# Two single PSUM banks for the third GEMM tile of the SSD mixer

## The chip, the cores and the metric

The kernel runs on one core of one Trainium2 chip. The metric is the device time of one execution in microseconds (us), taken as the median of several runs. The profile used here comes from one further execution of the same program, recorded by the hardware profiler. The engines are named as the profile names them: PE is TensorE (matrix products), PEld its weight loads, DVE is VectorE, ACT is ScalarE, POOL is GpSimd, and SP is SyncE, whose queue issues the DMAs.

## The reference

Two layers work on 512 latent tokens with 256 context tokens in front, at model width 1024, in fp32. Layer 0 mixes tokens by attention, layer 1 by a bidirectional Mamba-2 mixer (SSD). A gated convolutional FFN follows each. The change lies in the SSD mixer, which computes, cut to its core:

```
h_lat, h_ctx           # modulated RMS norms, 512 and 256 tokens x 1024
z, xbc, dt = split(h @ w_in, widths 2048, 4096, 64)
xbc = silu(dwconv_centred(xbc, w, b))   # 5 taps over positions, latent and context apart
x, B, C = split(xbc)                    # 32 heads of 64 in 8 groups, state of 128
dt = softplus(dt + bias);  a = -exp(a_log)
# in both directions, in chunks of 128 tokens:
h_t = exp(dt_t a) h_{t-1} + dt_t B_t x_t ;  y_t = C_t h_t
y = (y_fwd + y_bwd + D x) * silu(z)
out = rms_norm(y) @ w_out               # added through a gate to the stream
```

The context runs through the state only: it starts the recurrence of the latent tokens, and of x and B it needs all 768 positions, of C and z only the latent 512.

## The kernel before

Features lie on the 128 partitions and tokens along the free axis. An fp32 product is made of three passes (`mm3`): with input and weight each split into a high and a low part, the rows of TensorE with L105 multiply high by high, L106 the low input by the high weight, L108 the high input by the low weight. `load_w` brings one weight tile of 128x1024 from memory (`wst`, a DMA in SyncE's queue), ScalarE casts the high part (`wh`, L85), and VectorE subtracts it for the low part (`wl`, L87). All three buffers come from one rotation of ten.

A GEMM tile of the SSD input projection makes 128 output features from eight k-steps: for latent tokens 8 x 3 matmuls of 512 columns, for context 8 x 3 of 256. The result lies in PSUM. PSUM is given out by two pools: `S`, two tiles of two banks each (1024 columns), and `B`, four tiles of a single bank (512 columns), from which `Bank` takes. A tile of a pool can be taken again once what was in it has been read by its last reader.

The mixer begins with `first_tiles`, which computes two GEMM tiles while the preceding norm is still being finished: the time steps (`ps_dt`) and the first x tile (`ps_x0`). Both are `S` tiles, and the profile calls both `ps_first`. ScalarE then reads the time steps in four passes (L914 and L915, twice each, the rows `dte` and `dt`), VectorE and ScalarE make the softplus and its running sums (`acs`, L935 and L936). `inproj` runs over the 8 groups. For each group it makes the tiles x0, x1, B, C, z0 and z1, in that order; group 0 takes its x0 from `first_tiles`, so that its x1 is the third GEMM tile of the mixer. `gemm` takes an `S` tile for each, called `ps_in`, and computes the context part ahead of the latent part. With both `S` tiles taken by the time steps and x0, x1 of group 0 takes the one of the time steps.

`conv` evicts a tile: ScalarE copies the latent columns (L955) and, for x and B, the context columns (L957) into a padded buffer `raw`, of which there are two, multiplies by the middle tap (L958), VectorE adds the other four taps (L960), and ScalarE applies SiLU (L964). In group 0, after C, the sums of the time steps are transposed to tokens (`ps_dtT`, copied by VectorE at L1136 into `acsT` and `dtT`), spread by a product (`ps_end`, L1141), and turned into decays (`dec`, `dw`). `core` then works on a group: it transposes x (`ps_xt`, L1004) and B (`ps_bt`), weights x (`xw`, L1018), makes the products of C and B (`ps_cb`) and the states (`ps_st`, L1030), the decay masks `E`, and from them `ps_yo` and `ps_y`, while `inproj` already works on the next group.

Behind the groups comes the output projection: `ysplit` splits each gated tile into high and low parts (L1180 on ScalarE, L1181 on VectorE; `hhy` and `hly` for the first eight tiles, `yh` and `yl` for the rest), and `ps_wo` are its products. The FFN follows.

Outside attention the order on each engine isn't written out by hand. A list scheduler sets it from the dependencies and its estimates of durations, when the program is built; pools then assign the buffers, and each engine executes its instructions in the order given.

Of the kernel before, what the change touches and what calls it, by code (L numbers as in the profile page):

```python
# [17 lines left out]
L = 512  # L18
C = 256
T = L + C  # L20
# [47 lines left out]
def t3(g, name, dt=F32, n=T):  # L68
    return g.t3p.tile([P, n], dt, tag="t3", bufs=g.n3, name=name)
# [20 lines left out]
def load_w(g, dram, lo_engine="dve", pin=False):  # L90

    st = t4(g, "wst")
    wh = t4(g, "wh", F32R)
    wl = t4(g, "wl", F32R)
    g.nc.sync.dma_start(st, dram)
    split(g, st, wh, wl, lo_engine=lo_engine, pin=pin)
    return wh, wl


def mm3(g, w, outs, first, last):  # L100

    wh, wl = w
    mm = g.nc.tensor.matmul
    for out, (ah, al) in outs:
        mm(out, wh, ah, start=first, stop=False)  # L105
        mm(out, wh, al, start=False, stop=False)  # L106
    for out, (ah, al) in outs:
        mm(out, wl, ah, start=False, stop=last)  # L108
# [106 lines left out]
def follow(g, bi):  # L215

    if g.last_act is not None:
        g.tc.add_manual_dep(bi.ins, g.last_act.ins.name, mybir.DependencyInfo(
            mybir.DependencyClass.NoSync, mybir.DependencyReason.DATA), reason="order of tables")
    g.last_act = bi  # L220
# [81 lines left out]
def S(g, name):  # L302
    return g.ps.tile([P, 1024], F32, tag="S", bufs=2, name=name)


def Bank(g, name):
    return g.ps.tile([P, 512], F32, tag="B", bufs=4, name=name)
# [44 lines left out]
def gemm_in(g, tiles, h, off, segs):  # L352


    for run in segs:
        for ps, w in tiles:
            for k in range(KT):
                ks = slice(k * P, (k + 1) * P)
                mm3(g, (w[0][:, ks], w[1][:, ks]),
                    [(ps[:, off[i] + a : off[i] + b], tuple(t[:, a:b] for t in h[i][k])) for i, a, b in run],  # L360
                    k == 0, k == KT - 1)
                yield
# [6 lines left out]
def first_tiles(g, ws, norm, bg):  # L369

    ends = ending(norm.streams)
    tiles = [(S(g, "ps_first"), w) for w in ws]
    for _ in gemm_in(g, tiles, norm.h, (0, L), [[s] for s in ends]):
        next(bg, None)
    for _ in bg:
        pass
    return [ps for ps, _ in tiles]
# [498 lines left out]
def ssd(g, x, norm, wf, bg, close):  # L876


    nc, I, tc = g.nc, g.I, g.tc
    par = lambda name, j, rows=P: g.par[:rows, PC[name] + j : PC[name] + j + 1]  # L880
    h = norm.h
    ps_dt, ps_x0 = first_tiles(g, wf, norm, bg)
# [14 lines left out]
    def gemm(w, streams):  # L897
        ps = S(g, "ps_in")
        for _ in gemm_in(g, [(ps, w)], h, (0, L), [[(i, 0, (L, C)[i])] for i in streams]):
            pass  # L900
        return ps
# [3 lines left out]
    ps = ps_dt  # L905
# [45 lines left out]
    def conv(ps, j, both, cv):  # L951
        raw = raws[raw_n[0] % 2]
        raw_n[0] += 1
        n = TW if both else L
        nc.scalar.copy(raw[:, 2 : 2 + L], ps[:, :L])  # L955
        if both:
            nc.scalar.copy(raw[:, L + 4 : L + 4 + C], ps[:, L:T])  # L957
        nc.scalar.activation(cv, raw[:, 2 : 2 + n], AF.Identity, scale=par("sw2", j), bias=par("sb", j))  # L958
        for tap in (0, 1, 3, 4):
            i = nc.vector.scalar_tensor_tensor(cv, raw[:, tap : tap + n], par(f"sw{tap}", j), cv, ALU.mult, ALU.add)  # L960
            while late:
                g.tc.add_manual_dep(i.ins, late.pop().ins.name, mybir.DependencyInfo(
                    mybir.DependencyClass.NoSync, mybir.DependencyReason.DATA), reason="PSUM first")
        follow(g, nc.scalar.activation(cv, cv, AF.Silu))  # L964
        return cv
# [4 lines left out]
    def inproj(gi):  # L970

        G = Group()
        ld = lambda i: load_w(g, I["win"][6 * gi + i])
        G.x = []
        for j in range(2):
            ps = ps_x0 if gi == j == 0 else gemm(ld(j), (1, 0))
            G.x.append(conv(ps, 2 * gi + j, True, t3(g, "xf")))
            yield G
        for name, i, st in (("B", 2, (1, 0)), ("C", 3, (0,))):
            ps = gemm(ld(i), st)  # L980
            yield None
            setattr(G, name, conv(ps, 8 * i + gi, i == 2, t3(g, "Bf") if i == 2 else t2("Cf")))
            yield G
        G.z = []
        for j in range(2):
            ps = gemm(ld(4 + j), (0,))
            z = t2("z")
            follow(g, nc.scalar.activation(z, ps[:, :L], AF.Silu))
            G.z.append(z)
            yield G  # L990
# [129 lines left out]
    for gi in range(8):  # L1120
        i = -1
        for G in inproj(gi):
            if G is None:
                next(prev, None)
# [79 lines left out]
    for kp in range(8):  # L1204
        w = load_w(g, I["wout0"][kp])
        if kp == 4:
            ws, ps = wm(4), Bank(g, "ps_wo")
# [19 lines left out]
    for m in range(4, KT):  # L1227
# [5 lines left out]
        for seg in SEGS[0] if m == KT - 1 else [(0, 0, L)]:  # L1233
            _, a, b = seg
            if m > 4:
                ps = Bank(g, "ps_wo")[:, : b - a]
# [203 lines left out]
```

## Time and profile before

| | us |
|---|---|
| runs | 1898.59, 1896.82, 1892.41 |
| median | 1896.82 |
| profiled execution | 1896.57 |
| its span, first to last instruction | 1894.8 |
| PE busy | 1864.3 |
| DVE busy | 1315.9 |
| ACT busy | 811.8 |
| POOL busy | 302.6 |
| mean granted TensorE clock | 0.994 of full speed |

In a row of the timeline stand the start, the length, the engine, the line in the kernel, the operation, output and inputs by the names of the program, and a count if several like it follow; in brackets the idle time just ahead of it and the instruction that ended this. Several matmuls overlap in TensorE's pipeline, so the distance of their starts, not the length of a row, is what one of them takes. Lines of helpers (L85 to L108) stand for all their callers; the tile names tell these apart.

### The profile page before, as it was taken

How to read it: one execution, taken by the hardware profiler on the slowest of the kernel's cores; microseconds unless marked ns; L12 is line 12 of the kernel's file. 1: busy time of each engine (PE TensorE's matmuls, PEld its weight loads, DVE VectorE, ACT ScalarE, POOL GpSimd, SP SyncE). 2: the span in 40 equal slices, each digit the busy share in tenths (PEclk: the TensorE clock that was granted, in tenths of full speed). 3: DMA queues.
4: the chain of work that ended last, by engine and by line, in shares of the span. 5: the costliest groups of instructions: out<-in, count | busy, mean ns of one | idle time of the engine just before them, and what ended most of it. 6: DMA issues, size and time to landing. Idle time of an engine off the chain costs nothing.

```text
span 1894.8 us, 28684 instructions
## 1 busy us (share of the span) xinstructions
PE 1864.3 (98%) x11426; PEld 1549.6 (82%) x11426; DVE 1315.9 (69%) x1949; ACT 811.8 (43%) x1410; POOL 302.6 (16%) x266
## 2 busy tenths in 40 slices
PE   9999999999999999999999999999999999999999
PEld 7876565688888888888888888888888878888887
DVE  6587778688877776444477877777787466565655
ACT  4544443364221222222366676776666352323331
POOL 2241120040000000000041334444333210000000
PEclk9999999999999999999999999999999999999999
DMA  9232441115443553222224323334353223223232
GB/s 341 81 105 62 134 153 37 34 57 189 145 133 124 183 183 123 67 67 67 67 90 122 120 83 120 118 121 125 122 161 107 79 78 100 98 81 110 89 101 89
DMA packets 74070, 211.67 MB, mean 112 GB/s; under 512 B 9040, under 2 KB 14544, under 8 KB 73808
## 3 DMA queue, kind: packets, MB, share of 16 engines
q1 hardware_dynamic: 73936, 209.84, 33.7%
q8 instruction: 90, 1.47, 0.3%
q14 instruction: 44, 0.36, 0.1%
HBM read 198.79 MB, written 6.82 MB: 109 GB/s over the span
## 4 chain that ended last, share of the span: by engine, by line
PE 82%; DVE 10%; issue 4%; ACT 2%; POOL 1%; DMA 1%; POOLq 0%; SPq 0%; DVEq 0%; ACTq 0%
PE ps_up L106 10%; PE ps_up L108 10%; PE ps_up L105 10%; PE ps_d L105 6%; PE ps_d L106 6%; PE ps_d L108 6%; PE ps_in L108 4%; PE ps_in L106 4%; PE ps_in L105 4%; PE ps_s L672 2%; PE ps_o L636 2%; PE ps_st L1030 2%; DVE ht L281 1%; PE ps_wo L108 1%; PE ps_wo L105 1%
## 5 line engine op out<-in xcount | busy, mean ns | idle before, releaser
L87 DVE TENSOR_TENSOR wl<-wst,wh 128x1024 fp32r<-128x1024 f32 x207 | 259.8, 1255 | 235.9 <-PE ps_up L106 137.3
L85 ACT CAST wh<-wst 128x1024 fp32r<-128x1024 f32 x211 | 221.2, 1049 | 400.9 <-DMA wst<-in_wup 328.9
L106 PE MATMUL ps_up<-hlf,wh 128*128 128x512 f32 (+1 forms) x1008 | 357.0, 354 | 0.0
L108 PE MATMUL ps_up<-hhf,wl 128*128 128x512 f32 (+1 forms) x1008 | 356.8, 354 | 0.0
L105 PE MATMUL ps_up<-hhf,wh 128*128 128x512 f32 x1008 | 356.8, 354 | 0.0
L106 PEld LDWEIGHTS ps_up<-hlf,wh 128*128 128x128 f32 x1008 | 190.6, 189 | 26.3
L105 PEld LDWEIGHTS ps_up<-hhf,wh 128*128 128x128 f32 x1008 | 190.5, 189 | 26.5
L108 PEld LDWEIGHTS ps_up<-hhf,wl 128*128 128x128 f32 x1008 | 190.5, 189 | 26.4
L105 PE MATMUL ps_in<-hhs,wh 128*128 128x512 f32 (+1 forms) x560 | 204.4, 365 | 1.2 <-ACT dt L915 1.2
L106 PE MATMUL ps_in<-hls,wh 128*128 128x512 f32 (+1 forms) x560 | 199.4, 356 | 0.0
L108 PE MATMUL ps_in<-hhs,wl 128*128 128x512 f32 (+1 forms) x560 | 198.7, 355 | 0.0
L105 PE MATMUL ps_d<-hdh,wh 128*128 128x512 f32 (+1 forms) x568 | 193.5, 342 | 0.2 <-ACT hdh L85 0.2
L108 PE MATMUL ps_d<-hdh,wl 128*128 128x512 f32 (+1 forms) x568 | 193.4, 341 | 0.0
L106 PE MATMUL ps_d<-hdl,wh 128*128 128x512 f32 (+1 forms) x568 | 192.9, 340 | 0.3 <-DVE hdl L87 0.3
L781 DVE SCALAR_TENSOR_TENSOR X<-ps_d,mod,X 128x512 f32<-128x512 f32 (+1 forms) x224 | 124.5, 585 | 35.2 <-PE ps_d L108 35.0
L105 PEld LDWEIGHTS ps_in<-hhs,wh 128*128 128x128 f32 x560 | 105.9, 189 | 16.3 <-ACT dt L915 1.4
L106 PEld LDWEIGHTS ps_d<-hdl,wh 128*128 128x128 f32 x568 | 106.7, 188 | 14.8 <-DVE hdl L87 0.7
L108 PEld LDWEIGHTS ps_in<-hhs,wl 128*128 128x128 f32 x560 | 105.8, 189 | 14.8
L108 PEld LDWEIGHTS ps_d<-hdh,wl 128*128 128x128 f32 x568 | 106.7, 188 | 13.1
L105 PEld LDWEIGHTS ps_d<-hdh,wh 128*128 128x128 f32 x568 | 106.3, 188 | 13.6 <-ACT hdh L85 0.7
L106 PEld LDWEIGHTS ps_in<-hls,wh 128*128 128x128 f32 x560 | 106.0, 189 | 13.2
L675 ACT ACTIVATE pr<-ps_s 128x1024 f32<-128x1024 f32 x56 | 57.2, 1021 | 109.8 <-PE ps_s L674 104.6
(344 smaller groups left out, 3675.2 us busy)
## 6 DMA issues: line engine op xcount, KB each, us to landing
wst<-in_wup SPq DMA_DIRECT2D x88, 512.0 KB, 3.3
wada<-in_adaT SPq DMA_DIRECT2D x56, 512.0 KB, 3.3
wst<-in_win SPq DMA_DIRECT2D x48, 512.0 KB, 3.4
wst<-in_wdown SPq DMA_DIRECT2D x44, 512.0 KB, 3.9
E<-ad SPq DMA_DIRECT2D x64, 256.0 KB, 6.0
wada<-in_adaB SPq DMA_DIRECT2D x24, 512.0 KB, 4.2
ec<-ead SPq DMA_DIRECT2D x64, 128.0 KB, 5.0
wst<-in_wout SPq DMA_DIRECT2D x16, 512.0 KB, 3.4
```

The lines of the kernel that those rows point to most:

```text
L85: keep(nc.scalar.copy(hi, src))
L87: keep(eng.tensor_tensor(lo, src, _r(hi), ALU.subtract))
L105: mm(out, wh, ah, start=first, stop=False)
L106: mm(out, wh, al, start=False, stop=False)
L108: mm(out, wl, ah, start=False, stop=last)
L281: nc.vector.scalar_tensor_tensor(t[:, c0:c1], ap, g.moda[layer][ca][:, m, v : v + 1], rs[:, c0:c1], ALU.mult, ALU.mult)
L636: nc.tensor.matmul(po[S64[e], :n], v, pr[:, 512 * e + off : 512 * e + off + n], start=first, stop=last)
L672: nc.tensor.matmul(outs[e], kk[e][a][S64[e], k], b[S64[e], q], start=i == 0, stop=False)
L675: nc.scalar.activation(pr, ps, AF.Exp)
L781: nc.vector.scalar_tensor_tensor(ap, o[:, c0:c1], gate[:, m, v : v + 1], ap, ALU.mult, ALU.add)
L1030: nc.tensor.matmul(ps[:, d * 256 : (d + 1) * 256], Bt[:, t * P : (t + 1) * P], xw[d][t], start=t == ts[0], stop=t == ts[-1])
```

## The change

x1 of group 0 no longer takes an `S` tile. It takes two tiles of the `B` pool, one for the latent columns and one for the context columns, and its two parts are computed one after the other, the context first. `conv` takes such a pair too, and copies each part from its own bank. Both are called `ps_in1` in the code; in the order below `ps_in_9692` is the context part and `ps_in_9691` the latent part. Lines behind the first edit move by 1, behind the second by 7.

```
-        nc.scalar.copy(raw[:, 2 : 2 + L], ps[:, :L])
+        pl, pc = (ps[0], ps[1][:, :C]) if isinstance(ps, list) else (ps[:, :L], ps[:, L:T])
+        nc.scalar.copy(raw[:, 2 : 2 + L], pl)
         if both:
-            nc.scalar.copy(raw[:, L + 4 : L + 4 + C], ps[:, L:T])
+            nc.scalar.copy(raw[:, L + 4 : L + 4 + C], pc)
...
         for j in range(2):
-            ps = ps_x0 if gi == j == 0 else gemm(ld(j), (1, 0))
+            if gi == 0 and j == 1:
+                w, ps = ld(j), [Bank(g, "ps_in1"), Bank(g, "ps_in1")]
+                for i in (1, 0):
+                    for _ in gemm_in(g, [(ps[i], w)], h, (0, 0), [[(i, 0, (L, C)[i])]]):
+                        pass
+            else:
+                ps = ps_x0 if gi == j == 0 else gemm(ld(j), (1, 0))
             G.x.append(conv(ps, 2 * gi + j, True, t3(g, "xf")))
```

The scheduler sets another order from there on. On TensorE, where the last latent k-steps of the two first tiles stand (`hhs` and `hls` are the high and low parts of the normed input), the difference reads:

```order
 L108 MATMUL ps_first<-hhs_7_4729,wl 128x256
+L105 MATMUL ps_in_9692<-hhs_0_4731,wh 128x256
+L106 MATMUL ps_in_9692<-hls_0_4732,wh 128x256
 L105 MATMUL ps_first<-hhs_0_4715,wh 128x256 x2
+L108 MATMUL ps_in_9692<-hhs_0_4731,wl 128x256
+L105 MATMUL ps_in_9692<-hhs_1_4733,wh 128x256
+L106 MATMUL ps_in_9692<-hls_1_4734,wh 128x256
+L108 MATMUL ps_in_9692<-hhs_1_4733,wl 128x256
 L106 MATMUL ps_first<-hls_0_4716,wh 128x256
 L108 MATMUL ps_first<-hhs_0_4715,wl 128x256
```

Six matmuls of the context part of x1 now stand among the products of the first tiles; the other 18, and the latent part, follow behind the last of these.

On ScalarE, where x0, x1, B and C of group 0 are evicted, the order before (`xf` with L964 are the SiLUs of x0 and x1, `raw_9668` receives B, `raw_9669` C):

```order
L964 ACT_TABLE_LOAD
L964 ACTIVATE xf<-xf 128x770
L955 COPY raw_9668<-ps_in 128x512
L957 COPY raw_9668<-ps_in 128x256
L958 ACTIVATE Bf<-raw_9668,par 128x770
L964 ACTIVATE xf<-xf 128x770
L85 CAST wh<-wst 128x1024
L955 COPY raw_9669<-ps_in 128x512
L958 ACTIVATE Cf<-raw_9669,par 128x512
```

and now:

```order
L965 ACT_TABLE_LOAD
L965 ACTIVATE xf<-xf 128x770 x2
L956 COPY raw_9668<-ps_in 128x512
L958 COPY raw_9668<-ps_in 128x256
L956 COPY raw_9669<-ps_in 128x512
L959 ACTIVATE Bf<-raw_9668,par 128x770
L959 ACTIVATE Cf<-raw_9669,par 128x512
L85 CAST wh<-wst 128x1024
```

Both SiLUs have moved ahead of the copies of B and C, and the cast of a later weight behind them. On VectorE the eight taps of x0 and x1 (L960, now L961) stand together, where two weight subtractions (L87) stood among them; one of them is left behind the taps, then come the copies of `acsT` and `dtT`, and the taps of B and C follow.

On TensorE in the output projection, behind the last rows on `hhy7`, there stood before the products of the fifth output tile (`ps_wo_14138`), whose inputs `hhy0` to `hhy7` come from early groups:

```order
L108 MATMUL ps_wo_13876<-hhy7_14104,wl_14084 128x512
L105 MATMUL ps_wo_14138<-hhy0_13884,wh_14127 128x512
L106 MATMUL ps_wo_14138<-hly0_13885,wh_14127 128x512
L108 MATMUL ps_wo_14138<-hhy0_13884,wl_14128 128x512
L105 MATMUL ps_wo_14138<-hhy1_13900,wh_14127 128x512
```

and now the first tiles' products on the next split tile stand there:

```order
L108 MATMUL ps_wo_13878<-hhy7_14105,wl_14085 128x512
L105 MATMUL ps_wo_13877<-yh_14164,wh_14122 128x512
L106 MATMUL ps_wo_13877<-yl_14165,wh_14122 128x512
L108 MATMUL ps_wo_13877<-yh_14164,wl_14123 128x512
L105 MATMUL ps_wo_13877<-yh_14164,wh_14122 128x512
```

The rows of the fifth tile (now `ps_wo_14139`) begin eleven rows later.

## The prediction

> **What bounds the kernel now.** I read the page first, then the busy time by stretch, then the waits of TensorE in the SSD layer, and last the timeline at the places where the order moves.
>
> The page's first row, and the busy time in stretches (start:end, length, then busy us of PE, PEld, DVE, ACT, POOL, the granted clock, DMA share, GB/s). 991.4 is where the time-step and first x tiles end, 1420 the end of the last projections of the SSD layer, 1500 the start of its gated FFN:
>
> ```profile
> PE 1864.3 (98%) x11426; PEld 1549.6 (82%) x11426; DVE 1315.9 (69%) x1949; ACT 811.8 (43%) x1410; POOL 302.6 (16%) x266
> ...
> 991.40:1003.00 11.60, 10.36 (x65) 9.28 (x64) 9.19 (x14) 7.47 (x13) 0.00 (x0) 1.00 0.15 47
> 1003.00:1420.00 417.00, 414.55 (x2440) 358.75 (x2439) 318.16 (x367) 290.19 (x616) 158.98 (x136) 1.00 0.40 123
> 1420.00:1500.00 80.00, 78.69 (x385) 64.46 (x384) 54.93 (x71) 42.03 (x89) 27.57 (x24) 1.00 0.31 100
> 1500.00:1540.00 40.00, 35.94 (x233) 31.95 (x232) 25.23 (x51) 17.91 (x40) 7.53 (x9) 0.96 0.15 53
> 1540.00:1894.80 354.80, 351.43 (x1593) 291.22 (x1592) 207.53 (x326) 108.47 (x128) 0.00 (x0) 1.00 0.30 97
> ```
>
> TensorE is the bound: 98% busy, and the change leaves its instruction count alone, so only its idle time can be won. That is 1.24 us in the stretch of the third tile, 2.45 us in the following 417 us, 1.31 at the output projection, 4.06 as the FFN starts. What those in the SSD groups wait for (total, times, longest):
>
> ```profile
> PE ps_xt L1004 <- DVE xf L1107: 1.6, 6, 0.5
> PE ps_in L105 <- ACT dt L915: 1.2, 1, 1.2
> PE ps_end L1141 <- DVE acsT L1136: 0.8, 1, 0.8
> ```
>
> The middle row is the wait that the change addresses; it occurs once in the program.
>
> **Part 1: the removed wait and the moved context steps.** TensorE, start and length, in the timeline:
>
> ```profile
> 984.80 0.39 PE L106 MATMUL ps_first<-hls,wh 128*128 128x256 f32 x1 [0.65 <-DVE hls L291]
> ...
> 991.12 0.28 PE L106 MATMUL ps_first<-hls,wh 128*128 128x256 f32 x1
> 991.24 0.28 PE L108 MATMUL ps_first<-hhs,wl 128*128 128x256 f32 x1
> 992.76 0.39 PE L105 MATMUL ps_in<-hhs,wh 128*128 128x256 f32 x1 [1.24 <-ACT dt L915]
> ...
> 995.98 0.40 PE L106 MATMUL ps_in<-hls,wh 128*128 128x512 f32 x1
> 996.21 0.39 PE L108 MATMUL ps_in<-hhs,wl 128*128 128x512 f32 x1
> ```
>
> A 256-column matmul follows the last by 0.12 us, a 512-column one by 0.23. The x1 tile (24 of each: 24 x 0.12 + 24 x 0.23 = 8.4 us) begins with the context, which the order now puts in part ahead of the last latent steps of the first tiles: six matmuls, 6 x 0.12 = 0.72 us, around 984.8, where 0.65 us is idle. They fill it: 0.65 gained. The other 18 follow without the wait for L915: 1.24 gained. x1 so ends 1.89 us earlier, at 992.76 + 8.4 - 1.89 = 999.3 instead of 1001.2. Its two copies remain two copies on ScalarE, at no cost while ScalarE there has waits of its own.
>
> **Part 2: the next wait for a double bank.** B, C and z0 still take double banks in turn; z0 takes the one of B, free once ScalarE has copied B. ScalarE, VectorE and TensorE there:
>
> ```profile
> 1012.24 0.85 ACT L964 ACTIVATE xf<-xf 128x770 f32<-128x770 f32 x1
> 1013.00 0.57 ACT L955 COPY raw<-ps_in 128x512 f32<-128x512 f32 x1
> 1013.46 0.38 ACT L957 COPY raw<-ps_in 128x256 f32<-128x256 f32 x1
> ```
> ```profile
> 1005.39 1.02 DVE L960 SCALAR_TENSOR_TENSOR xf<-raw,par,xf 128x770 f32<-128x770 f32 x1
> 1006.33 1.22 DVE L87 TENSOR_TENSOR wl<-wst,wh 128x1024 fp32r<-128x1024 f32 x1
> 1007.46 5.67 DVE L960 SCALAR_TENSOR_TENSOR xf<-raw,par,xf 128x770 f32<-128x770 f32 x6
> 1013.05 1.22 DVE L87 TENSOR_TENSOR wl<-wst,wh 128x1024 fp32r<-128x1024 f32 x1
> 1014.19 1.02 DVE L960 SCALAR_TENSOR_TENSOR xf<-raw,par,xf 128x770 f32<-128x770 f32 x1
> ...
> 1017.11 0.55 DVE L1136 COPY acsT<-ps_dtT 128x384 f32<-128x384 f32 x1
> ...
> 1029.33 3.03 DVE L1018 TENSOR_TENSOR xw<-xt,dw 128x512 f32<-128x512 f32 x4
> ```
> ```profile
> 1014.99 0.49 PE L1135 MATMUL ps_dtT<-cst,acs 128*128 128x128 f32 x3
> ...
> 1015.56 0.48 PE L105 MATMUL ps_in<-hhs,wh 128*128 128x512 f32 x1
> ...
> 1017.72 0.92 PE L1141 MATMUL ps_end<-acsT,cst 128*128 128x192 f32 x4 [0.75 <-DVE acsT L1136]
> ...
> 1031.35 1.89 PE L1030 MATMUL ps_st<-xw,Bt 128*128 128x256 f32 x8
> ```
>
> Before, ScalarE copies B at 1013.00 between the two SiLUs of x0 and x1. The new order puts both SiLUs ahead of the copies, and the second one needs all eight taps of VectorE. The taps still begin at 1005.39 (the time-step chain, which the change leaves alone, sets that) and now run without the weight subtraction between: 8 x 5.67/6 = 7.56, to 1012.95. Then a SiLU at its pitch of 0.76 (1012.24 to 1013.00), a copy at 0.46 and one of 0.38: the double bank is free at 1014.55. TensorE would be there at 999.3 + 8.4 (B) + 24 x 0.23 (C) + 0.57 (the six transposes ahead of z0, 1014.99 to 1015.56) = 1013.8. A new wait of about 0.8 us, and z0 starts at 1014.55, 1.0 us earlier than before: part of the gain is given back here.
>
> acsT is now copied before the taps of B, right behind the one subtraction that follows the eight taps (1.14, from 1013.05 to 1014.19): 1012.95 + 1.14 + 0.55 = 1014.6. ps_end, one k-step into z0, finds it ready, so its 0.75 us goes too: 1.0 + 0.75 = 1.75 us ahead.
>
> Behind that TensorE meets ps_st, which needs xw. The xw chain hangs on the SiLUs, a table load and the decays behind the taps of C, which begin after the copies: 1014.55 + 0.57 + 1.03 + 8 taps, some 0.3 us earlier than before and not 1.75. The first quarter of xw was done at 1029.33 + 3.03/4 = 1030.1, the second at 1030.85, and ps_st began at 1031.35 without a wait. At 1031.35 - 1.75 = 1029.6 it is 0.2 to 0.9 too early for the same two, 0.3 earlier each. I take 0.5, between these, and net about 1.2 us go into the second group. Later groups have waits of 0.5 us at most, and these are latencies of their own work (ps_xt on L1107), so I carry 1.2 on; the bounds are 0.3 (all caught by xw) and 1.9 + 0.75 + 1.6 = 4.2 (nothing given back, and the six ps_xt waits lost as well).
>
> **Part 3: the output projection.** The order also differs 450 us later. There TensorE multiplied 26 rows of the fifth output tile, whose inputs were long ready, while y of the last group was split into yh (L1180) and yl (L1181); now the rows on the new yh stand first.
>
> ```profile
> 1450.20 1.22 DVE L87 TENSOR_TENSOR wl<-wst,wh 128x1024 fp32r<-128x1024 f32 x1
> ...
> 1450.46 0.39 PE L105 MATMUL ps_wo<-hhy,wh 128*128 128x512 f32 x1
> ...
> 1450.86 2.55 ACT L1180 ACTIVATE yh<-z,par 128x512 fp32r<-128x512 f32 x4
> ...
> 1451.47 0.50 PE L108 MATMUL ps_wo<-hhy,wl 128*128 128x512 f32 x1 [0.40 <-DVE wl L87]
> ...
> 1451.60 3.50 DVE L1181 SCALAR_TENSOR_TENSOR yl<-z,par,yh 128x512 fp32r<-128x512 f32 x4 [0.18 <-ACT yh L1180]
> ```
>
> TensorE reaches the first yh row at 1450.46. The first yh is ready at 1450.86 + 2.55/4 = 1451.5: 1.0 us. The first yl is ready at 1451.60 + 3.50/4 = 1452.5, and its row stands one pitch of 0.23 behind 1451.5: 0.8 more. The low part of the fifth tile's weight now follows the four yl (1451.60 + 3.50 + 1.22 = 1456.3); its row, 16 pitches behind 1452.5, comes at 1456.2: 0.1. So 1.9 us of waits where 0.40 was: a loss of 1.5. Bounds: 0 (y ready sooner) and 3.5 (the whole yl batch).
>
> **Part 4: weights and the FFN's start.** A load takes the buffer that a product four weights back leaves, where most waited for a subtraction two weights back. The lead left is about three products (17 to 25 us at 5.5 to 8.4 each), against this chain, from the page (mean ns of a subtraction and of a cast; us to landing of a load):
>
> ```profile
> L87 DVE TENSOR_TENSOR wl<-wst,wh 128x1024 fp32r<-128x1024 f32 x207 | 259.8, 1255 | 235.9 <-PE ps_up L106 137.3
> L85 ACT CAST wh<-wst 128x1024 fp32r<-128x1024 f32 x211 | 221.2, 1049 | 400.9 <-DMA wst<-in_wup 328.9
> ...
> wst<-in_win SPq DMA_DIRECT2D x48, 512.0 KB, 3.4
> ```
>
> 3.4 + 1.05 + 1.26 = 5.7 us: covered, unless SyncE's queue holds a load back by over 11 us. I put it at 0, with 7 us as the far end (below). The FFN's start has 4.06 us idle with the neighbours on VectorE slightly rearranged; ±1 us, taken as 0. The stretch within it where the clock dips, and the longest wait in that stretch:
>
> ```profile
> 1521.00:1530.00 9.00, 7.06 (x40) 6.45 (x41) 8.00 (x17) 7.12 (x17) 3.06 (x3) 0.81 0.17 60
> ```
> ```profile
> 1524.68 0.39 PE L106 MATMUL ps_first<-hlf,wh 128*128 128x256 f32 x1 [1.03 <-POOL hlf L288]
> ```
>
> Short waits, 1.94 us idle in nine, came with a granted clock of 0.81: 9 x 0.19 = 1.7 us of clock lost. The 1.9 us of new waits in part 3 fall in six, so a similar dip may cost up to 1.7 more, and the upper end keeps that; yet the 1.24 us wait kept 1.00, so the sum has 0. The Trainium skill ("TensorE: Matmul & The Clock Gate", section "What's actually happening") says the array falls to half clock after at least one idle window of about 3.4 us. By that rule no wait here would cost any clock; the trace differs, since this dip came with idle time spread over waits of 1.03 us and less.
>
> **Sum.** 1896.57 (profiled execution: span 1894.8 and 1.8 around it) - 1.2 + 1.5 = 1896.9 us, 0.1 above the median of the three runs shown. Those spread by 6.2 us; 0.3%, 5.7 us, is about what a measurement can tell from no change, so the cases part at 1891.1 and 1902.5.
>
> **The rivals.** *Faster:* nothing is given back. 4.2 us and the FFN's 1.7 us of clock also saved make 5.9: 1890.7. For it: every one of these waits stands in the trace. Against it: z0's bank and xw, whose own chains move by little. Chance 0.15. *The wait only changes its name:* all is caught at z0 and xw (gain 0.3), the projection unchanged: 1896.3 to 1897.8. This lies inside the forecast's band, with it 0.52. *Slower:* the load order through SyncE. Each later load stands behind the row broadcasts of the previous group and now waits for a whole product. If the slack of 11 us is used up, one weight a group comes late; seven groups at 1 us each, on top of the sum: 1903.9; at 1.5 us, 1907.4. For it: queues move in every group from the second on, and I bounded rather than followed each. Against: 11 us is much. With the projection's upper bound of 3.5 and its clock dip of 1.7 (together 5.2 - 1.2 = 4.0, 1900.6) little is needed to pass 1902.5. Chance 0.33.
>
> **How the numbers follow.** The likeliest is no measurable change, 1896.9, with its own range 1893 (4.2 less) to 1901. The range reaches into both rivals: 1890 to 1907.
>
> **What would show it.** Right: no wait of ps_in on L915; a new wait of ps_in on ScalarE's copy near 1014, about 0.8; ps_end without a wait; ps_wo waiting on yh and yl, 1.9 us in all. Wrong: waits on wl or wh in groups two to eight, a granted clock under 1.00 in the projection, or z0 starting by 1013.8.

## The result, and the profile after

The changed kernel takes 1900.49 us (median of 21 runs, 1896.57 to 1907.88), the kernel before 1896.90 (21 runs, 1891.80 to 1900.91, on the same chips). The ratio is 1.0028, 95% interval [1.0019, 1.0038]: slower by 0.28%, some 5 us. A second comparison of the same two kernels gave 1900.25 against 1895.74, ratio 1.0021 [1.0011, 1.0032]. The ratios, here and below, are not the quotients of the two medians and differ from these by up to 0.1% (here 1.0019 and 1.0024, or 3.6 and 4.5 us). The profiled execution took 1904.09 us, its span is 1902.3.

The page's first row of the changed kernel; the row of before stands in the prediction:

```profile
PE 1867.0 (98%) x11426; PEld 1551.6 (82%) x11426; DVE 1324.1 (70%) x1949; ACT 811.3 (43%) x1410; POOL 302.8 (16%) x266
```

The work is the same, instruction for instruction in number. DVE has become busier by 8.2 us: some of its instructions take longer.

What TensorE waits for in the changed kernel (total us, times, longest), in four stretches: 940 to 1060 (head of the mixer and the first group), 1060 to 1420 (the other groups), 1420 to 1505 (output projection), 1505 to 1550 (start of the FFN). Lines behind the edit are those of before plus 7.

```profile
PE ps_bt L1018 <- ACT Bf L965: 1.4, 1, 1.4
...
PE ps_in L105 <- ACT raw L958: 0.9, 1, 0.9
...
PE ps_in L108 <- DVE wl L87: 0.2, 1, 0.2
...
PE ps_xt L1011 <- DVE xf L1114: 1.8, 5, 0.7
PE ps_xt L1011 <- DVE ec L1104: 1.3, 1, 1.3
PE ps_cb L1056 <- ACT Cf L965: 0.6, 1, 0.6
...
PE ps_y L1111 <- ACT E L1074: 1.3, 1, 1.3
PE ps_wo L106 <- DVE yl L1188: 1.1, 1, 1.1
PE ps_y L1111 <- DVE E L1086: 0.3, 1, 0.3
...
PE ps_first L105 <- ACT hhf L290: 2.7, 2, 1.5
PE ps_first L106 <- POOL hlf L288: 1.7, 2, 1.4
PE ps_first L106 <- DVE hlf L291: 0.5, 1, 0.5
```

The wait of ps_in on L915 (1.2) and that of ps_end (0.8) are gone, and the forecast one on ScalarE's copy (L958) stands there with 0.9. New are ps_bt on the SiLU of B (1.4), ps_xt on L1104 (1.3, which is the step that reads `ps_yo` of the group before), ps_cb on the SiLU of C (0.6), ps_wo on yl, and more in the rows of the FFN.

Where the time goes shows best at marks along TensorE. Each number is the start of the product named (in the last three rows the end), less that of before, both counted from the mixer's first product. The part ahead of the mixer, which the change leaves alone, is taken out this way; between the executions of this table it differs by up to 5 us. The kernels of the other columns are those of the experiments.

| us, less the kernel before | changed | changed, again | pool_hold | banks_new_head | banks_old_order |
|---|---|---|---|---|---|
| ps_dtT (all of x1, B, C done) | -2.1 | -2.0 | -2.0 | -2.0 | -1.4 |
| ps_end | -2.5 | -2.4 | -2.4 | -2.4 | +0.1 |
| ps_bt, group 0 | -0.4 | -0.3 | -1.5 | -1.5 | +0.1 |
| ps_cb, group 0 | 0.0 | 0.0 | -1.6 | -1.6 | +0.1 |
| ps_bt, group 1 | +0.5 | +0.5 | -0.9 | +0.9 | +0.1 |
| ps_bt, group 2 | +1.6 | +1.6 | +0.2 | +0.9 | +0.2 |
| ps_bt, group 3 | +2.3 | +2.3 | +0.9 | +0.9 | +0.2 |
| ps_wo, first | +2.8 | +2.7 | +1.3 | +1.4 | +0.3 |
| ps_wo, last | +4.2 | +4.0 | +2.6 | +1.5 | +0.3 |
| FFN's first tiles done | +5.9 | +4.7 | +4.3 | +1.2 | +0.3 |
| end | +6.2 | +5.0 | +4.6 | +1.6 | +0.6 |

Two marks of the first four columns don't compare like with like. Ahead of ps_end the new order has two products of z0 where there were five, and ahead of ps_bt of group 0 it has one product of z1 more. At 0.23 us each, TensorE's lead is 1.8 us at ps_end (of the 2.5, 0.7 is work put off) and 0.6 at ps_bt. At all other marks of these columns the same products are done. The kernel before, from z0 to ps_end:

```profile
1015.56 0.48 PE L105 MATMUL ps_in<-hhs,wh 128*128 128x512 f32 x1
1015.88 0.39 PE L106 MATMUL ps_in<-hls,wh 128*128 128x512 f32 x1
1016.11 0.39 PE L108 MATMUL ps_in<-hhs,wl 128*128 128x512 f32 x1
1016.34 0.40 PE L105 MATMUL ps_in<-hhs,wh 128*128 128x512 f32 x1
1016.58 0.39 PE L106 MATMUL ps_in<-hls,wh 128*128 128x512 f32 x1
1017.72 0.92 PE L1141 MATMUL ps_end<-acsT,cst 128*128 128x192 f32 x4 [0.75 <-DVE acsT L1136]
```

So in the changed kernel 1.8 us are won by ps_end, and all of it is lost again by the first group's C-by-B product. The groups then lose 2.8, the projection 1.4, and the FFN's start 0.7 to 1.7.

The first loss, in the timeline of the changed kernel: TensorE, VectorE's taps of B and C, and GpSimd's masks on E. Two of the taps in the kernel before, for comparison:

```profile
1017.58 1.01 DVE L960 SCALAR_TENSOR_TENSOR Bf<-raw,par,Bf 128x770 f32<-128x770 f32 x1
1018.51 0.74 DVE L960 SCALAR_TENSOR_TENSOR Cf<-raw,par,Cf 128x512 f32<-128x512 f32 x1
```

The changed kernel:

```profile
1015.96 0.50 PE L105 MATMUL ps_in<-hhs,wh 128*128 128x512 f32 x1 [0.91 <-ACT raw L958]
1016.30 0.39 PE L106 MATMUL ps_in<-hls,wh 128*128 128x512 f32 x1
1016.52 0.81 PE L1148 MATMUL ps_end<-acsT,cst 128*128 128x192 f32 x4
...
1025.29 0.88 PE L1018 MATMUL ps_bt<-cst,Bf 128*128 128x128 f32 x6 [1.41 <-ACT Bf L965]
```
```profile
1018.30 0.74 DVE L961 SCALAR_TENSOR_TENSOR Cf<-raw,par,Cf 128x512 f32<-128x512 f32 x1
1018.96 1.02 DVE L961 SCALAR_TENSOR_TENSOR Bf<-raw,par,Bf 128x770 f32<-128x770 f32 x1
1019.89 1.12 DVE L961 SCALAR_TENSOR_TENSOR Cf<-raw,par,Cf 128x512 f32<-128x512 f32 x1
1020.93 1.38 DVE L961 SCALAR_TENSOR_TENSOR Bf<-raw,par,Bf 128x770 f32<-128x770 f32 x1
1022.24 0.74 DVE L961 SCALAR_TENSOR_TENSOR Cf<-raw,par,Cf 128x512 f32<-128x512 f32 x1
1022.90 1.46 DVE L961 SCALAR_TENSOR_TENSOR Bf<-raw,par,Bf 128x770 f32<-128x770 f32 x1
1024.28 1.11 DVE L961 SCALAR_TENSOR_TENSOR Cf<-raw,par,Cf 128x512 f32<-128x512 f32 x1
```
```profile
1019.60 0.87 POOL L1070 TENSOR_SCALAR_AFFINE_SELECT E<-E 128x512 f32<-128x512 f32 x1 [31.25 <-DMA E<-ad]
1020.65 0.85 POOL L1070 TENSOR_SCALAR_AFFINE_SELECT E<-E 128x512 f32<-128x512 f32 x1 [0.19 <-DMA E<-ad]
1022.91 1.94 POOL L1070 TENSOR_SCALAR_AFFINE_SELECT E<-E 128x512 f32<-128x512 f32 x2 [1.41 <-DMA E<-ad]
```

Four of the taps take longer by 0.36 to 0.44 us, 1.55 in all, and they are those that begin while a mask runs or together with one. (The tap at 1018.96, during which the first mask begins, takes 1.02 as without.) They make 1.55 of the 8.2 us by which VectorE is busier; whether the rest bears on the later losses was not tested. In the kernel before the masks come 14 us later, behind all these taps. Why, tells SyncE's queue (the broadcasts of E's rows and the first mask before, the broadcasts after):

```profile
1007.75 21.20 SPq L95 DMA_DIRECT2D wst<-in_win  x4
1029.01 5.01 SPq L1062 DMA_DIRECT2D E<-ad  x8
...
1033.28 0.70 POOL L1063 TENSOR_SCALAR_AFFINE_SELECT E<-E 128x512 f32<-128x512 f32 x1 [46.26 <-PE ps_st L1030]
```
```profile
1008.54 5.98 SPq L95 DMA_DIRECT2D wst<-in_win  x3
1014.95 6.08 SPq L1069 DMA_DIRECT2D E<-ad  x8
```

Before, weight loads held up the queue until their buffers came free, the last of them until 1028.6, and the broadcasts stood behind them. Now eight loads of the input projection stand ahead of the broadcasts (three in the row above, five earlier) where there were ten (four and six), and the broadcasts go out 14 us earlier. The first mask follows the first broadcast by 4.3 us before and by 4.7 now, so it is the broadcast that it waits for, though the row of before names ps_st.

### The profile page after: what moved, and what is told of

Read it like the earlier page. It is cut to its first block, busy times and chain, and to the rows that moved or that the text cites. A ratio compares the mean times of both kernels' runs of the same rounds, so it can differ in the third digit from the quotient of the medians.

```text
span 1902.3 us, 28681 instructions
## 1 busy us (share of the span) xinstructions
PE 1867.0 (98%) x11426; PEld 1551.6 (82%) x11426; DVE 1324.1 (70%) x1949; ACT 811.3 (43%) x1410; POOL 302.8 (16%) x266
## 4 chain that ended last, share of the span: by engine, by line
PE 81%; DVE 10%; issue 3%; DMA 3%; ACT 2%; POOL 0%; SPq 0%; POOLq 0%; DVEq 0%; ACTq 0%
PE ps_up L108 10%; PE ps_up L106 10%; PE ps_up L105 10%; PE ps_d L105 6%; PE ps_d L106 6%; PE ps_d L108 6%; PE ps_in L108 4%; PE ps_in L106 4%; PE ps_in L105 4%; PE ps_o L636 2%; PE ps_s L672 2%; PE ps_st L1037 2%; DVE ht L281 1%; DVE xf L961 1%; PE ps_wo L106 1%
## 5 line engine op out<-in xcount | busy, mean ns | idle before, releaser
L87 DVE TENSOR_TENSOR wl<-wst,wh 128x1024 fp32r<-128x1024 f32 x207 | 260.9, 1261 | 231.4 <-PE ps_up L106 139.6
L106 PE MATMUL ps_up<-hlf,wh 128*128 128x512 f32 (+1 forms) x1008 | 357.0, 354 | 0.0
L105 PE MATMUL ps_up<-hhf,wh 128*128 128x512 f32 x1008 | 356.8, 354 | 0.0
L106 PEld LDWEIGHTS ps_up<-hlf,wh 128*128 128x128 f32 x1008 | 190.6, 189 | 26.4
L105 PEld LDWEIGHTS ps_up<-hhf,wh 128*128 128x128 f32 x1008 | 190.5, 189 | 26.4
L105 PE MATMUL ps_in<-hhs,wh 128*128 128x512 f32 (+1 forms) x560 | 204.1, 364 | 0.9 <-ACT raw L958 0.9
L106 PE MATMUL ps_in<-hls,wh 128*128 128x512 f32 (+1 forms) x560 | 199.4, 356 | 0.0
L105 PE MATMUL ps_d<-hdh,wh 128*128 128x512 f32 (+1 forms) x568 | 193.5, 342 | 0.2 <-ACT hdh L85 0.2
L106 PE MATMUL ps_d<-hdl,wh 128*128 128x512 f32 (+1 forms) x568 | 192.9, 340 | 0.3 <-DVE hdl L87 0.3
L105 PEld LDWEIGHTS ps_in<-hhs,wh 128*128 128x128 f32 x560 | 105.9, 189 | 15.9 <-ACT raw L958 1.1
L106 PEld LDWEIGHTS ps_d<-hdl,wh 128*128 128x128 f32 x568 | 106.7, 188 | 14.8 <-DVE hdl L87 0.7
L105 PEld LDWEIGHTS ps_d<-hdh,wh 128*128 128x128 f32 x568 | 106.3, 188 | 13.6 <-ACT hdh L85 0.6
L106 PEld LDWEIGHTS ps_in<-hls,wh 128*128 128x128 f32 x560 | 106.0, 189 | 13.3
```

What stands on the lines that cost most here:

```text
L87: keep(eng.tensor_tensor(lo, src, _r(hi), ALU.subtract))
```

## The experiments

**Theory 1:** the time comes from the order that the scheduler sets once a double bank is no longer needed, not from the banks; (1a) in the first group it is GpSimd's early masks that slow VectorE's taps, or (1b) something else in that order. **Theory 2:** the two single banks that x1 takes are missed by others that use the same four. **Theory 3:** only the dips of the granted clock at the FFN's start differ, by chance. The table speaks against it as the main cause: 4.2 and 4.0 us stand at the last row of the projection, ahead of these dips. To part bank and order, `pin` gives each engine a list of the order in which to issue; it adds edges of order, no waits between engines. In the fences below the comment behind `pin` says what is in the list. "Head" is the mixer up to the decays and `xw` of group 0, "groups" the seven others, "tail" the output projection and the start of the FFN. Each kernel ran beside the kernel before, in five rounds.

**The banks with the old order** (the changed kernel, each engine in the order of the kernel before):

```
+    pin(nc, tc)      # head, groups and tail: order of the kernel before
```

> x1 of group 0 in the two single banks, as in the changed kernel, but every engine keeps the issue order of the kernel before. Theory 1 (the order that the scheduler makes costs the time, the banks do not): the 1.24 us wait on the time steps goes, but in the old order ps_end still waits for acsT, whose place on VectorE did not move, so 0.75 becomes about 2.0 us; the time is that of before, within 1 us. Theory 2 (x1 holds two of the four single banks, and what needs these comes late): as slow as the changed kernel, 3.6 to 5.3 us over before, with new PE waits in the first groups. Theory 3 (only half-clock windows at the FFN's start differ by chance): no difference from before beyond 1 us, and none between any of these four.

1894.94 us against 1895.15, ratio 1.0004 [0.9995, 1.0013]. Its waits of TensorE from 984 to 1420:

```profile
PE ps_end L1148 <- DVE acsT L1143: 2.3, 1, 2.3
PE ps_xt L1011 <- DVE xf L1114: 1.8, 6, 0.5
```

The wait for the eviction is gone and the tile ends 1.4 us earlier, but the next wait, that of ps_end on a copy of VectorE, grows from 0.8 to 2.3. Nothing is won and nothing is lost, within the interval (0.9 us faster to 2.5 slower): in the old order the banks as such cost nothing that can be measured, and theory 2 falls for it.

**The old banks with the new tail** (the kernel before, x1 in its double bank):

```
+    pin(nc, tc)      # head and groups: old order; tail: order of the changed kernel
```

> x1 in a double bank as before; the order of before up to the end of the groups, and from the output projection on the order of the changed kernel, on every engine. Theory 1: 1.1 to 1.5 us of waits on yl and yh in the projection in place of 0.4, so 1 us slower than before, and up to 1.7 more if the FFN's start falls into a second half-clock window: +1 to +2.7 us. Theory 2: the time of before. Theory 3: the time of before within 1 us.

1896.54 against 1895.15, ratio 1.0009 [1.0000, 1.0018]. The wait on yl (1.1) and the longer ones at the FFN's start (2.7, 1.7, 0.5) are there. The trace is behind the kernel before by 0.6 us at the last row of the projection, 1.2 behind the FFN's first tiles and 1.6 at the end, with a wait of 1.0 of ps_cb at the joint of the two orders in it. The tail's order costs of the order of 1.5 us here, not more. Most of it falls at the FFN's start: from ps_bt of group 6 to the last row of the projection this kernel loses only 0.3 us, since TensorE comes late enough from the joint not to wait for ps_y (0.9 before). So the 1.4 us that the changed kernel loses in the projection are not the cost of the projection's order whatever comes ahead of it.

**The old banks with the new groups and tail:**

```
+    pin(nc, tc)      # head: old order; groups and tail: order of the changed kernel
```

> x1 in a double bank as before and the old order through the first tiles, z0 and the decays of group 0; from the second group on the order of the changed kernel, on every engine. Theory 1: the groups lose 2.5 to 3.2 us (a ps_xt wait of 1.3 us behind VectorE's ec in the third group, ps_cb waiting for Cf), the projection its 1 to 1.5: +4 to +6 us over before, as slow as the changed kernel or slower. Theory 2: the time of before. Theory 3: the time of before within 1 us.

1905.55 against 1895.15, ratio 1.0062 [1.0048, 1.0075]: about twice what was expected. The excess is made at the joint: on VectorE a weight subtraction still stands ahead of xw as in the old order, but its cast on ScalarE follows the new one, behind the SiLUs of z and the copy of C by B. TensorE's longest wait, the subtraction, and the stretch:

```profile
PE ps_st L1030 <- DVE xw L1018: 4.4, 1, 4.4
...
1032.76 1.23 DVE L87 TENSOR_TENSOR wl<-wst,wh 128x1024 fp32r<-128x1024 f32 x1 [6.01 <-ACT wh L85]
...
1020.00:1060.00 40.00, 35.61 (x182) 30.76 (x181) 19.73 (x28) 26.80 (x74) 13.23 (x14) 0.91 0.30 100
1060.00:1080.00 20.00, 20.00 (x139) 17.21 (x137) 19.59 (x22) 11.30 (x15) 2.01 (x1) 1.00 0.23 75
```

With the wait of 4.4 us comes a loss of 40 x 0.09 = 3.6 us of clock, part of it while TensorE stands. By B of group 1 it is 7.5 us behind; from there it loses 1.8 up to group 5 (1.3 of it the wait of ps_xt on L1104), then 1.35 in the projection, as the changed kernel does (2.2 and 1.4). So the loss of the groups behind the first comes with their order and doesn't need the banks; the total says nothing, because of the joint.

**The banks with the new head alone:**

```
+    pin(nc, tc)      # head: order of the changed kernel; groups and tail: old order
```

> x1 in single banks with the new order of the first tiles, of x0 to z0 and of the decays; from the second group on the order of before on every engine. Theory 1: 2.5 us ahead at ps_end, but ps_bt then waits 1.4 us for B and the rest is lost by ps_cb, so between 0.5 us faster than before and the same. Theory 2: 3.6 to 5.3 us slower than before. Theory 3: as before within 1 us.

1898.01 against 1895.15, ratio 1.0010 [0.9995, 1.0025]. No gain came, and not by the way expected: ps_bt doesn't wait 1.4 us for B. Here the place of E's broadcasts is that of the old order, behind ten weight loads, and they issue at 1029.35; with no mask beside them the taps take 1.02 and 0.75, ps_bt waits 0.2, and 1.6 us are won at ps_cb of group 0. In group 1 the kernel loses 2.5 again:

```profile
PE ps_xt L1011 <- DVE xf L1114: 3.9, 7, 1.8
```

ps_xt needs the bank of ps_y that VectorE reads at L1114. By the code that chain starts with the masks, and these are no earlier than before (the first 70.5 us behind the mixer's first product, 70.3 before); that this is why the wait grows was not tested. What TensorE wins in the head it waits for at a later point that hangs on VectorE.

**The changed kernel with GpSimd held back:** its first mask of group 0 waits for the last tap of C. All else is the changed kernel, its order included. (The fence is shortened: the two names stand for numbers of instructions.)

```
+    pin(nc, tc)      # order of the changed kernel
+    tc.add_manual_dep(first_mask, last_tap_of_C, Sync)
```

> The changed kernel with its own issue order on every engine, but GpSimd's first mask of group 0 (affine select, L1070) has to wait until VectorE has done the last tap of C. In the changed kernel four masks ran between 1019.6 and 1024.9 and the taps of B and C beside them took 1.12, 1.38, 1.46 and 1.11 us, where the same ones take 0.74 and 1.02 otherwise. Theory 1a (the masks slow the taps, and so B and the weighted x): the taps take 0.74 and 1.02 again, the 1.4 us wait of ps_bt shrinks to about 0.2, ps_cb comes 1.2 to 1.5 us earlier than in the changed kernel, and the whole is 0.5 to 1.5 us faster than it. Theory 1b (ps_bt waits because B was copied out late, whatever GpSimd does): taps and wait stay, and the masks, 4 us later, cost another 1 us or more in group 1.

1898.75 against 1895.88, ratio 1.0018 [1.0006, 1.0030]. Its taps, masks and ps_bt:

```profile
1016.91 1.01 DVE L961 SCALAR_TENSOR_TENSOR Bf<-raw,par,Bf 128x770 f32<-128x770 f32 x1
1017.84 0.74 DVE L961 SCALAR_TENSOR_TENSOR Cf<-raw,par,Cf 128x512 f32<-128x512 f32 x1
1018.50 1.01 DVE L961 SCALAR_TENSOR_TENSOR Bf<-raw,par,Bf 128x770 f32<-128x770 f32 x1
1019.43 0.74 DVE L961 SCALAR_TENSOR_TENSOR Cf<-raw,par,Cf 128x512 f32<-128x512 f32 x1
```
```profile
1020.48 3.09 POOL L1070 TENSOR_SCALAR_AFFINE_SELECT E<-E 128x512 f32<-128x512 f32 x4 [35.77 <-DMA E<-ad]
```
```profile
1020.45 0.88 PE L1018 MATMUL ps_bt<-cst,Bf 128*128 128x128 f32 x6 [0.21 <-ACT Bf L965]
```

(The first broadcast was issued at 1011.30 here; what the mask waited for is the tap that ends at 1019.43 + 0.74 = 1020.17.) With the same order and no mask beside them the taps are back at 1.01 and 0.74, and the wait of ps_bt falls from 1.4 to 0.2. Of a lead of 1.7 us at ps_end (2.4 by the mark) 1.6 is left at ps_cb, where the changed kernel has none. 1a is shown for the first group, 1b falls. The 1.5 us stay won to the last row of the projection (+2.6 where the changed kernel had +4.2); the groups behind lose their 2.8 with the hold too, so the masks of the first group are not what costs there. In the ratio the intervals of the two overlap, so what the hold is worth is read from the trace.

**The same with the old order from group 2 on, and the changed kernel with the old order from group 2 on** (no hold):

```
+    pin(nc, tc)      # head and group 1: order of the changed kernel; from group 2 on: old order
```

> As the run with the held mask, and from group 2 on every engine has the order of the kernel before (projection and FFN too). Theory 1a with theory 1 (the loss of the changed kernel lies in the later order): 1.5 us ahead of before at ps_cb of group 0, 0.5 of it lost in group 1, nothing after: 1 us faster than before (1895.9 where before is 1896.9). If something in group 1 ties the groups to another engine's chain, the lead is lost there by waits of ps_xt for a bank, and the time is that of before or up to 1.5 us over it.

> The changed kernel's order through group 1, without any hold, and the order of before from group 2 on, on every engine. Theory 1: level with before at ps_cb of group 0, 0.5 us behind at the end of group 1, and no more after: 0.5 us over before, where the whole changed kernel is 3.6 to 5.3 over; the difference is what the order of groups 2 to 7, the projection and the FFN's start cost. If the two single banks or the first groups were the cause, it stays 3 us or more over before.

1906.73 against 1895.88, ratio 1.0067 [1.0052, 1.0082], and 1907.88, ratio 1.0069 [1.0056, 1.0082]. Both expectations missed, for one reason. Up to B of group 1 they stand where they should (-1.0 with the hold and +0.3 without). At the joint of the orders both have

```profile
PE ps_yo L1102 <- DVE hs L1047: 7.3, 3, 4.4
```

and lose 11 us by B of group 2, some of it clock (0.83 over 1110 to 1140 in the second). They tell nothing about the rest of the groups, except that two orders, each sound, can't be joined just anywhere.

**The copy of acsT ahead of the taps of B**, with the banks and the old order elsewhere: if ps_end's wait is all that takes the gain, it should stay won.

```
 VectorE:
+L1143 COPY acsT<-ps_dtT 128x384
 L961 SCALAR_TENSOR_TENSOR Bf<-raw,par,Bf 128x770 x2
-L1143 COPY acsT<-ps_dtT 128x384
```

> x1 in single banks and the order of before on every engine, with one step moved: VectorE copies acsT ahead of the taps of B instead of behind the first two. Theory 1: the 2.3 us wait of ps_end shrinks to about 0.2, so TensorE is 2 us ahead there; xw, which hangs on the decays behind the taps of C, is not earlier, so ps_st takes 1 to 1.9 us of it back, and 0 to 0.5 us remain at the end: 1896.4 to 1896.9 where before is 1896.9. If the lead is kept, 2 us faster than before.

1896.87 against 1895.88, ratio 1.0003 [0.9994, 1.0012]: nothing that can be measured, as expected. ps_end waits 0.3 and starts 1.9 us earlier; right behind it stands a new wait:

```profile
PE ps_xt L1011 <- ACT xt L1012: 1.1, 1, 1.1
```

At ps_cb of group 0 0.75 us is left, at the first row of the projection 0.3, at the end none.

**The changed kernel once more**, next to the others:

> The changed kernel itself, run beside the next one: 0.2 to 0.4% over before (3.6 to 7 us), as on record.

1900.25 against 1895.74, ratio 1.0021 [1.0011, 1.0032]. The marks of the table agree within 0.2 us with the first trace up to the last row of the projection.

**With the hold, and in group 2 the step that frees ps_yo earlier:** one L1104 and one L1114 ahead of the last two taps of B on VectorE.

```
 VectorE, group 2:
+L1114 SCALAR_TENSOR_TENSOR xf<-xf,par,ps_y 128x512
+L1104 TENSOR_TENSOR ec<-ec,ps_yo 128x512
 L961 SCALAR_TENSOR_TENSOR Bf<-raw,par,Bf 128x770 x2
-L1104 TENSOR_TENSOR ec<-ec,ps_yo 128x512
-L1114 SCALAR_TENSOR_TENSOR xf<-xf,par,ps_y 128x512
```

> The changed kernel's order with GpSimd's first mask held until the last tap of C (as in the run with the hold), and in group 2 VectorE reads ps_yo and ps_y (one L1104 and one L1114) ahead of the last two taps of B instead of behind them. Theory 1: the 1.3 us wait of ps_xt for the bank that L1104 reads goes, without a new one, so 1.3 us less than with the hold alone (which was 0.18% over before): 0.1% over before, and 0.15 to 0.2% under the changed kernel beside it. If TensorE is tied there by another chain, a wait of the same size appears on ps_bt or ps_cb of the same group, and the time stays at that of the hold alone.

1898.73 against 1895.74, ratio 1.0017 [1.0008, 1.0027], as with the hold alone; the gain that theory 1 expected did not come, its alternative did. The wait of 1.3 on L1104 is gone, and in the same group there is another:

```profile
PE ps_cb L1056 <- ACT Cf L965: 1.7, 2, 1.1
```

ps_bt of group 2 comes 1.4 us ahead of the kernel before and ps_cb 0.2 ahead. The taps that were moved back are now what TensorE waits for. At this place VectorE's chain of taps and evictions binds TensorE, whichever of these two steps comes first.

## Why the prediction was right or wrong

The measured 1900.49 lies in the range, and that is in good part luck: the range of 1890 to 1907 reached into both rivals, while the lead that the sum carried to the end was lost in the first group already. The slowdown of 0.28% is just inside the 0.3% below which I called it the same, but its interval leaves out zero: the sum had +0.1 us and the chip shows about 5 (5.3 and 4.0 by the two ratios, 5.0 by the second trace).

- Part 1, right. 1.89 us forecast, 2.1 by ps_dtT.
- Part 2, right up to ps_end. The new wait of z0 on the double bank of B was 0.91 (0.8 forecast), z0 starts 0.9 us earlier (1.0), ps_end waits no more, and the lead there, without the three products put off, is 1.8 (1.75).
- Part 2, what is given back: the term that was mis-sized. I took 0.5 us, at ps_st, and at most 1.45 (1.75 down to the lower bound of 0.3). The measured loss is all of the 1.8, and it begins earlier: 1.2 of it at ps_bt, the rest by ps_cb. I carried over the taps' durations from before to an order in which GpSimd works beside them. The broadcasts of E do stand in SyncE's queue, and I weighed that queue for the weights only; that fewer loads ahead of them send the masks among the taps I did not follow. `pool_hold` shows that this makes 1.5 us of the 1.8: with the hold hardly 0.2 is given back, less than my 0.5.
- "I carry 1.2 on", wrong in sign. I said that the groups' waits are latencies of their own work and bounded their part by nothing lost. They lose 2.8 us, of which the rows show 2.1: 1.3 at L1104, 0.6 at L965, 0.2 more at L1114. `double_new_groups` shows 2.0 of it, from B of group 1 on, without the banks; `pool_hold_ec_first` shows that removing one of these waits calls up the next.
- Part 3, right in size (1.5 forecast, 1.4 measured), in part by luck. The row on yl came 1.3 us late, but the first on yh, for which I had 1.0, hardly waited (1455.87, against 1455.83 by the pitch); a wait that I did not have, of ps_y ahead of them, grew by 0.7. The fifth tile has 24 rows there, not 26; nothing in the sum hangs on it.
- Part 4. Weights at 0: right, 0.2 us at L87, and that one only in the first group, where the hold removes it too. The FFN's start at 0 ±1 with up to 1.7 of clock: +0.7 in the second trace of the changed kernel, with the clock's loss as before, and +1.7 in the first, with twice that loss. The rows of ps_first there wait 4.9 us in all, for 3.4 before (L105 2.1, L106 1.3). That comes with the tail's order, since `double_new_projection` has the same 2.7, 1.7 and 0.5; which step of it stays open.
- The rivals. "Slower by the load order through SyncE" had the queue right and its victim wrong: no weight of the later groups was late. "The wait only changes its name" is what the change does with the order held (`banks_old_order`, `acst_early`).

How the 2.8 us of the groups divide over the orders of the single engines was not settled; the stalls at the joints of the mixed orders cover it. So the cause is shown by experiment for the first group's 1.5 us; for the rest it is shown that it comes with the order, not which step of it.

## What to carry to other kernels

Removing a wait from the engine that bounds a kernel is worth only the slack up to the next wait on an engine that is no earlier: here the time won went to ps_end in the old order, to ps_bt in the new one, and to ps_xt where these two were out of the way. Where a scheduler sets the order, the change of order it brings can weigh more than the wait (here 5 us against 1.2): price each queue that moves, and above all what an engine begins earlier, since its work may land beside that of a neighbour and slow it. To part a resource from the order, hold the order and change the resource alone; don't join two orders in the middle of a pipeline.

## What the runs showed of the hardware

VectorE's taps, which read two tensors from SBUF, took 1.38 to 1.46 us where they began beside a mask of GpSimd, and 1.01 to 1.02 without one; those of 512 columns 1.11 to 1.12 and 0.74. The masks suffer too: the first two took 0.87 and 0.85 us and the next two 1.94 together, where one by itself takes 0.63, as this one of the kernel before:

```profile
1039.84 0.63 POOL L1063 TENSOR_SCALAR_AFFINE_SELECT E<-E 128x512 f32<-128x512 f32 x1 [0.20 <-DMA E<-ad]
```

The Trainium skill ("SBUF — State Buffer", section "Who interferes with whom") says that a VectorE instruction with two SBUF inputs contends with a GpSimd instruction that reads SBUF, and that the port pair which the two engines share is an exclusive lock. The trace agrees that such a pair collides; each tap lost 0.36 to 0.44 us, less than the 0.63 of a mask.

The stretch of the FFN's start in which the clock dips, in the changed kernel's first trace (columns as in the prediction):

```profile
1527.00:1539.00 12.00, 9.16 (x50) 8.76 (x51) 9.22 (x20) 6.70 (x17) 4.52 (x4) 0.72 0.14 45
```

12 x 0.28 = 3.4 us of clock are lost here, twice the 1.7 before, with 2.84 us idle and no wait of over 1.5. Within the stretch the clock is 0.50 for 6.8 us; in the second trace of the changed kernel, with the same waits, for 3.4. In `banks_new_head`, whose waits there are those of the kernel before (1.8 us on hhf, 1.6 on hlf), it stays at 1.00. So the waits alone don't decide whether the clock dips, and what does stays open. The wait of 2.3 us in `banks_old_order` cost no clock (the marks behind it stay at +0.1), while the clock dips where the waits of 4.4 us stand in three other kernels (0.91 over 1020 to 1060 in `double_new_groups`, 0.87 and 0.83 over 1110 to 1140 in the two that go over to the old order at group 2). The Trainium skill ("TensorE: Matmul & The Clock Gate", section "What's actually happening") names an idle window of about 3.4 us as the condition; the waits of 4.4 us agree with that, the dip at the FFN's start does not.
